# A depthwise convolution over two streams: the taps of both in one instruction, and eight of 31 on the tensor engine

## The chip, the cores and the metric

The kernel runs on one NeuronCore of a Trainium2 chip. Its engines work side by side from their own instruction queues: TensorE (matrix products; PE in the profile, PEld for its weight loads), VectorE (DVE), ScalarE (ACT), GpSimd (POOL) and SyncE (SP, which here issues the DMAs). The metric is the device time of one execution in microseconds, taken as the median of several runs.

## The reference, cut to what matters

The program is a whole model in float32: a block with two layers (a latent stream of 512 tokens and a context stream of 256 tokens, width 1024) and behind it a second block with two layers. The change lies in the first mixer of the first block. It projects both streams, and a quarter of the projection goes through a depthwise convolution of width 31 over time, each stream by itself with zeros at its ends:

```python
def conformer_conv(p_glu, conv_w, conv_b, ln_g, ln_b):
    a, gate = jnp.split(p_glu, 2, axis=-1)
    u = depthwise_conv(a * jax.nn.sigmoid(gate), conv_w, conv_b)   # 31 taps, 512 channels
    return jax.nn.silu(layer_norm(u, ln_g, ln_b))
```

Its result and that of a differential attention are put side by side and projected back to width 1024. The convolution is thus 31 multiplications and additions for each of 512 channels and 768 tokens; its result is first needed by the output projection, which comes after the attention has begun.

## The kernel before

**Layout.** Channels lie on the 128 partitions, tokens along the free axis. The 512 convolution channels are four blocks (`i` = 0 to 3), the two streams are `regs` (`r` = 0: 512 columns, `r` = 1: 256 columns). The convolution's input `us` holds, for each block, both streams in one row of 828 columns, each with 15 zeros on either side, so that stream 1 begins 30 columns later than in an array without zeros. Large products are made in three passes (lines 90 to 92): weights and activations are split into a high half and a low remainder (`whi`, `wlo`), the high half cast by ScalarE (line 73), the low one subtracted by VectorE or GpSimd (line 74).

**The stages around the change.** First come the gate gemms (lines 412 to 424): for each block, two gemms per stream give gate and value, and VectorE writes `us` (line 420) and starts the result `conv` with the first tap and the bias (line 421). The filters of a later Hyena layer (`hyena_filters`) are made in the same stage. Then the loop of line 488 makes eight query/key gemms, each followed on VectorE by three instructions of a rotation (lines 493 to 495); the loop of line 500 makes the value gemms. Between these, one step at a time by `next(tg)`, runs the generator `taps` (line 436), and after its eight steps the four of `conv_norm` (line 456, layer norm and activation). Attention follows (from line 539), with the first half of the output projection as filler (`out_gemm(0, ...)`), which reads the convolution's result.

**The taps.** For each block and stream: ScalarE multiplies taps 30 and 29 into two buffers, GpSimd adds these, VectorE does taps 1 to 28 one after the other in place, and GpSimd adds its part:

```python
for j in range(1, 29):
    nc.vector.scalar_tensor_tensor(out=o, in0=u[:, j:j + n], scalar=cw[:, i, j:j + 1], in1=o,
                                   op0=ALU.mult, op1=ALU.add)                    # lines 448 to 450
nc.gpsimd.tensor_tensor(out=o, in0=o, in1=o2, op=ALU.add)                        # line 451
```

**The modulation.** While the query/key and value weights are loaded, `wsplit` (line 60) also advances a generator (`k.mods`, line 141): eight weights of 512 KB per kind, each with two products into 32 of the 128 rows of one accumulator (line 153), a copy by ScalarE (line 157), a second accumulator (line 160) and an addition by VectorE (line 161). Its weights and those of the gemms share three raw buffers (`wraw`, lines 66 and 149).

**Order.** Each engine works through its queue in a fixed order. The framework writes that order when the program is built: it goes through the instructions by their order in the program as priority, with a time model of its own, and lets a later instruction go first where an earlier one cannot start yet in that model. So taps are mixed into the gate stage too. On the chip the order stays as written, even where the times come out otherwise.

**Accumulators.** PSUM has eight banks. Lines 370, 371, 374 and 485 deal them out: four for the gemms (`evps`), two for the modulation (`evmps`), two for the Hyena filters and, after these, for the norm of the convolution (`evcps`). The pool `evp` (line 435) opens when the Hyena filters' pools are closed and reuses their memory, a tile at a time.

Of the kernel before, what the change touches and what calls it, by code (L numbers as in the profile page):

```python
# [10 lines left out]
F32 = mybir.dt.float32  # L11
# [15 lines left out]
def f32(ap):  # L27
    return ap.bitcast(F32)

# [325 lines left out]
def even_mixer(k, xc):  # L355
# [10 lines left out]
    with ExitStack() as es:  # L366
# [3 lines left out]
        ps = hp.enter_context(k.pool("evps", 4, space=PSUM))  # L370
        mps = hp.enter_context(k.pool("evmps", 2, space=PSUM))
        lam = cp.tile([128, 1], F32, name="lam")
        conv = [k.tmp([128, TC], "conv", F32, 4, cp) for i in range(4)]
        with k.pool("hyf") as hy, k.pool("evf", 2, space=PSUM) as fps:
# [5 lines left out]
            with k.pool("evn") as np_:  # L380
                rbs = [k.norm_stats([t], [rg], ps, np_)[0] for t, rg in zip((xl, xc), regs)]
                with k.pool("ada", side="right") as mp:
                    for i, _ in enumerate(chain(k.mods(0, 1, mps, mp, 12), k.mods(0, 0, mps, mp, 12))):
                        if i == 3:
                            next(fg)
                h1 = hp.enter_context(k.pool("evh", side="right"))
                hh = h1.tile([128, 8, TC], F32R, name="hh")
                hl = h1.tile([128, 8, TC], F32R, name="hl")
                h = (hh, hl)
                k.norm([xl, xc], regs, [k.mgain(0, 1, G_N1, r) for r in range(2)], [k.mcol(0, 0, r) for r in range(2)], hh, hl, ps, np_, rbs)  # L390
# [14 lines left out]
            with k.pool("evu") as pp:  # L405
# [6 lines left out]
                for i in range(4):  # L412
                    ws = [k.wsplit(a["ev_w_fm"][i * 2 + j]) for j in range(2)]
                    for r, (c0, n) in enumerate(regs):
# [6 lines left out]
                        nc.vector.tensor_scalar(out=conv[i][:, c0:c0 + n], in0=us[:, i, u0 - 15:u0 - 15 + n], scalar1=cw[:, i, 0:1],  # L421
                                                scalar2=cb[:, i:i + 1], op0=ALU.mult, op1=ALU.add)
                        next(fg, None)
                    next(fg, None)
# [9 lines left out]
        qk = [b3() for i in range(8)]  # L434
        with k.pool("evp") as pp, k.behind([k.mods(0, kind, mps) for kind in (2, 3, 4)], 2):
            def taps():

                for i in range(4):
                    for r, (c0, n) in enumerate(regs):
                        u = us[:, i, c0 + 30 * r:c0 + 30 * r + 30 + n]  # L440
                        o = conv[i][:, c0:c0 + n]
                        o2 = k.tmp([128, T], "cv2", bufs=2, pool=tp_)[:, :n]
                        nc.scalar.mul(o2, u[:, 30:30 + n], cw[:, i, 30:31])
                        for j in (29,):
                            o3 = k.tmp([128, T], "cv3", bufs=2, pool=tp_)[:, :n]
                            nc.scalar.mul(o3, u[:, j:j + n], cw[:, i, j:j + 1])
                            nc.gpsimd.tensor_tensor(out=o2, in0=o2, in1=o3, op=ALU.add)
                        for j in range(1, 29):
                            nc.vector.scalar_tensor_tensor(out=o, in0=u[:, j:j + n], scalar=cw[:, i, j:j + 1], in1=o,
                                                           op0=ALU.mult, op1=ALU.add)  # L450
                        nc.gpsimd.tensor_tensor(out=o, in0=o, in1=o2, op=ALU.add)
                        yield
                for r in range(2):
                    yield from conv_norm(r)

            def conv_norm(r):
                c0, n = regs[r]
                cs = [conv[i][:, c0:c0 + n] for i in range(4)]
# [26 lines left out]
            cps = hp.enter_context(k.pool("evcps", 2, space=PSUM))  # L485
# [53 lines left out]
        with k.pool("eva") as pp, k.pool("evaps", 2, space=PSUM) as ps, k.pool("evop", 1, space=PSUM) as op_, k.pool("evgp", 1, space=PSUM) as gp, \  # L539
# [88 lines left out]
            for i in range(4):  # L628
                k.split(conv[i], mix[2 * i], mix[2 * i + 1])
# [3 lines left out]
            for u, (hd, c0, k0) in enumerate(units):  # L633
# [4 lines left out]
                if u % 3 == 0:  # L638
                    os_ = k.tmp([128, TC], "conv", F32, 4, cp)
# [1609 lines left out]
```

## Time and profile before

| | |
|---|---|
| median of 3 runs | 3670.63 us (3670.61 to 3671.2) |
| the profiled execution | 3667.19 us |
| its span, first to last instruction | 3665.4 us |
| mean granted clock of TensorE | 0.970 |
| TensorE busy | 3410.3 us |
| VectorE busy | 2439.1 us |
| ScalarE busy | 1464.3 us |
| GpSimd busy | 680.0 us |

The span is what the profile shows; the time of the execution has 1.8 us more around it. The profile names an instruction by its line, engine, operation and tiles (output <- inputs), with partitions x elements. Times of a timeline are from the span's start. A granted clock of 1.0 is 2.4 GHz, 0.5 is 1.2 GHz. A product of float32 operands shows as two records of TensorE. The convolution's stage lies between 75 and 370 us of the span; everything behind it is as long as ten such stages.

### The profile page before, as it was taken

How to read it: one execution, taken by the hardware profiler on the slowest of the kernel's cores; microseconds unless marked ns; L12 is line 12 of the kernel's file. 1: busy time of each engine (PE TensorE's matmuls, PEld its weight loads, DVE VectorE, ACT ScalarE, POOL GpSimd, SP SyncE). 2: the span in 40 equal slices, each digit the busy share in tenths (PEclk: the TensorE clock that was granted, in tenths of full speed). 3: DMA queues.
4: the chain of work that ended last, by engine and by line, in shares of the span. 5: the costliest groups of instructions: out<-in, count | busy, mean ns of one | idle time of the engine just before them, and what ended most of it. 6: DMA issues, size and time to landing. Idle time of an engine off the chain costs nothing.

```text
span 3665.4 us, 55031 instructions
## 1 busy us (share of the span) xinstructions
PE 3410.3 (93%) x21924; PEld 2813.6 (77%) x21924; DVE 2439.1 (67%) x4107; ACT 1464.3 (40%) x2529; POOL 680.0 (19%) x595
## 2 busy tenths in 40 slices
PE   6985989999998899889999999999999989999999
PEld 3764878888887666567888887767998777777998
DVE  7998877554448855654333676667877676758886
ACT  4212643213226434323223444544444554644443
POOL 0034201002102432311111032022111032012110
PEclk9997999999999999989999999999999999999999
DMA  6333113333333222422222313332333313242333
GB/s 212 109 127 93 48 50 117 119 125 118 120 111 110 89 71 78 125 97 81 92 93 97 107 59 101 97 121 83 103 106 97 116 50 115 77 132 83 102 98 98
DMA packets 156843, 369.32 MB, mean 101 GB/s; under 512 B 19207, under 2 KB 44167, under 8 KB 156200
## 3 DMA queue, kind: packets, MB, share of 16 engines
q1 hardware_dynamic: 156584, 365.79, 31.3%
q8 instruction: 172, 2.82, 0.3%
q14 instruction: 87, 0.71, 0.1%
HBM read 334.27 MB, written 28.31 MB: 99 GB/s over the span
## 4 chain that ended last, share of the span: by engine, by line
PE 39%; DVE 14%; issue 7%; ACT 4%; POOL 2%; DMA 2%; SPq 0%; DVEq 0%; POOLq 0%; ACTq 0%
PE acc L90 11%; PE acc L92 11%; PE acc L91 10%; DVE wlo L74 2%; DMA wraw<-in_w_up_dram 2%; DVE wslo L85 1%; DVE hb L1612 1%; ACT whi L73 1%; PE rec L1337 1%; PE rec L1338 1%; DVE ws L1920 1%; PE rec L1322 1%; DVE oz L828 1%; ACT mp L1847 0%; DVE xl L2023 0%
## 5 line engine op out<-in xcount | busy, mean ns | idle before, releaser
L73 ACT CAST whi<-wraw 128x1024 fp32r<-128x1024 f32 (+2 forms) x442 | 408.0, 924 | 843.3 <-PE acc L91 652.9
L74 DVE TENSOR_TENSOR wlo<-wraw,whi 128x1024 fp32r<-128x1024 f32 (+2 forms) x438 | 490.5, 1120 | 184.7 <-ACT whi L73 180.5
L90 PE MATMUL acc<-hh,whi 128*128 128x512 f32 (+1 forms) x1024 | 367.2, 359 | 10.8 <-ACT whi L73 7.6
L92 PE MATMUL acc<-hh,wlo 128*128 128x512 f32 (+1 forms) x1024 | 364.4, 357 | 6.9 <-DVE wlo L74 4.0
L91 PE MATMUL acc<-hl,whi 128*128 128x512 f32 (+1 forms) x1024 | 365.6, 357 | 2.5 <-DVE hl L256 2.1
L91 PE MATMUL acc<-hidl,whi 128*128 128x512 f32 (+1 forms) x768 | 274.3, 357 | 2.9 <-DVE hidl L85 2.9
L90 PE MATMUL acc<-hidh,whi 128*128 128x512 f32 (+1 forms) x768 | 274.6, 358 | 0.0
L92 PE MATMUL acc<-hidh,wlo 128*128 128x512 f32 (+1 forms) x768 | 274.2, 357 | 0.0
L341 POOL TENSOR_TENSOR sqr<-relu 128x512 f32<-128x512 f32 (+1 forms) x96 | 126.6, 1319 | 688.9 <-ACT relu L339 675.6
L90 PEld LDWEIGHTS acc<-hh,whi 128*128 128x128 f32 x1024 | 195.9, 191 | 49.9 <-ACT whi L73 11.5
L92 PEld LDWEIGHTS acc<-hh,wlo 128*128 128x128 f32 x1024 | 195.4, 191 | 39.9 <-DVE wlo L74 6.1
L91 PEld LDWEIGHTS acc<-hl,whi 128*128 128x128 f32 x1024 | 196.5, 192 | 35.8 <-DVE hl L256 5.6
L92 PE MATMUL acc<-shh,wlo 128*128 128x512 f32 (+1 forms) x480 | 193.6, 404 | 7.6 <-DVE wlo L74 7.6
L90 PE MATMUL acc<-shh,whi 128*128 128x512 f32 (+1 forms) x480 | 195.6, 407 | 3.5 <-ACT whi L73 3.5
L91 PE MATMUL acc<-shl,whi 128*128 128x512 f32 (+1 forms) x480 | 194.1, 404 | 0.2 <-issue 0.2
L85 POOL TENSOR_TENSOR flo<-fth,fhi 128x512 fp32r<-128x512 f32 x44 | 84.9, 1931 | 530.1 <-ACT fhi L84 473.6
L90 PE MATMUL acc<-fsh,wshi 128*128 128x256 f32 x576 | 163.5, 284 | 4.5 <-ACT wshi L84 4.5
L91 PEld LDWEIGHTS acc<-hidl,whi 128*128 128x128 f32 x768 | 145.5, 189 | 26.9 <-DVE hidl L85 3.4
L191 DVE SCALAR_TENSOR_TENSOR mdacc<-wraw,cs,mdacc 128x1024 f32<-128x1024 f32 x70 | 94.4, 1372 | 103.7 <-DMA wraw<-in_ada_w_dram 103.6
L91 PE MATMUL acc<-fsl,wshi 128*128 128x256 f32 x576 | 163.2, 283 | 0.0
L90 PEld LDWEIGHTS acc<-hidh,whi 128*128 128x128 f32 x768 | 144.8, 188 | 23.5
L92 PEld LDWEIGHTS acc<-hidh,wlo 128*128 128x128 f32 x768 | 144.8, 189 | 23.2
(684 smaller groups left out, 9167.8 us busy)
## 6 DMA issues: line engine op xcount, KB each, us to landing
wraw<-in_mlp_w_dram SPq DMA_DIRECT2D x128, 512.0 KB, 3.5
wraw<-in_ada_w_dram SPq DMA_DIRECT2D x96, 512.0 KB, 4.0
wraw<-in_w_in_dram SPq DMA_DIRECT2D x58, 512.0 KB, 3.5
wraw<-in_od_w_fm_dram SPq DMA_DIRECT2D x36, 512.0 KB, 3.5
wraw<-in_w_gate_dram SPq DMA_DIRECT2D x72, 256.0 KB, 2.9
wraw<-in_w_up_dram SPq DMA_DIRECT2D x72, 256.0 KB, 3.1
wraw<-in_w_down_dram SPq DMA_DIRECT2D x48, 256.0 KB, 2.7
wraw<-in_w_down_dram SPq DMA_DIRECT2D x32, 320.0 KB, 3.0
```

What stands on the lines that cost most here:

```text
L73: nc.scalar.copy(hi, raw)
L74: (eng or nc.vector).tensor_tensor(out=lo, in0=raw, in1=f32(hi), op=ALU.subtract)
L85: (eng or nc.vector).tensor_tensor(out=lo, in0=src, in1=f32(hi), op=ALU.subtract)
L90: nc.tensor.matmul(out, s[0], m[0], start=first, stop=False)
L91: nc.tensor.matmul(out, s[0], m[1], start=False, stop=False)
L92: nc.tensor.matmul(out, s[1], m[0], start=False, stop=last)
L191: nc.vector.scalar_tensor_tensor(out=acc, in0=w, scalar=c, in1=acc, op0=ALU.mult, op1=ALU.add)
L341: nc.gpsimd.tensor_tensor(out=s, in0=r, in1=r, op=ALU.mult)
L828: nc.vector.scalar_tensor_tensor(out=o, in0=p[:, j:j + n], scalar=w[:, j:j + 1], in1=o, op0=ALU.mult, op1=ALU.add)
L1322: nc.tensor.matmul(vn_ps[pf[d], hd], wT[:, c, pf[d]], S[:, c], start=True, stop=True)
L1337: nc.tensor.matmul(op_[pf[d], hd], qd[:, c, pf[d]], S[:, c], start=True, stop=False)
L1338: nc.tensor.matmul(op_[pf[d], hd], at[pf[d], c], vn[pf[d], hd], start=False, stop=True)
```

## The change

The result `conv` gets 798 columns instead of 768, so that it lies like the input: both streams with 30 columns between them, which are computed and never read. One tap is then one instruction over both streams. Taps 1 to 20 stay with VectorE, 29 and 30 with ScalarE and GpSimd, and taps 21 to 28 (`P0, PT = 21, 8`) go to TensorE. For these GpSimd makes, per block and tap, a matrix of 128 x 32 (`dia`) that holds a 32x32 diagonal for each quarter of the channels. `strips` multiplies each quarter `q` of the channels by its diagonals into its own bank; four taps `s` go to the four quarters of the bank's rows, and two rounds of 16 products accumulate. ScalarE copies the four banks out, and `joined` sums the four taps of each bank by four products with a 128x32 matrix of ones on the diagonals (`k.sum4`); VectorE adds that to `conv`.

The banks are dealt anew: three for the gemms, two for the modulation at first and one afterwards (`evmps1`), four for the strips and the norm. The buffers of the ScalarE taps move to the pool `evp`, and the first tap with the bias is done once per block over both streams. Readers of `conv` take its columns per stream.

```diff
-        ps = hp.enter_context(k.pool("evps", 4, space=PSUM))
-        mps = hp.enter_context(k.pool("evmps", 2, space=PSUM))
+        ps = hp.enter_context(k.pool("evps", 3, space=PSUM))
+        W = TC + 30
+        conv = [k.tmp([128, W], "conv", F32, 4, cp) for i in range(4)]
...
-                with k.pool("ada", side="right") as mp:
+                with k.pool("ada", side="right") as mp, k.pool("evmps", 2, space=PSUM) as mps:
...
-                        nc.vector.tensor_scalar(out=conv[i][:, c0:c0 + n], in0=us[:, i, u0 - 15:u0 - 15 + n], scalar1=cw[:, i, 0:1],
-                                                scalar2=cb[:, i:i + 1], op0=ALU.mult, op1=ALU.add)
                         next(fg, None)
+                    nc.vector.tensor_scalar(out=conv[i], in0=us[:, i, 0:W], scalar1=cw[:, i, 0:1], scalar2=cb[:, i:i + 1], op0=ALU.mult, op1=ALU.add)
...
+        mps = hp.enter_context(k.pool("evmps1", 1, space=PSUM))
+        cps = hp.enter_context(k.pool("evcps", 4, space=PSUM))
...
+            dia = pp.tile([128, 4, PT, 32], F32, name="cdia")
+            for i in range(4):
+                nc.gpsimd.tensor_tensor(out=dia[:, i], in0=k.sum4.unsqueeze(1).to_broadcast([128, PT, 32]),
+                                        in1=cw[:, i, P0:P0 + PT].unsqueeze(2).to_broadcast([128, PT, 32]), op=ALU.mult)
+            def strips(i, r):
+                c0, n = regs[r]
+                bank = [k.tmp([128, 512], "acc", pool=cps, bufs=None) for _ in range(4)]
+                for t in range(0, PT, 4):
+                    for s in range(4):
+                        for q in range(4):
+                            p = slice(32 * q, 32 * q + 32)
+                            u0 = c0 + 30 * r + P0 + t + s
+                            nc.tensor.matmul(bank[q][32 * s:32 * s + 32, :n], dia[p, i, t + s], us[p, i, u0:u0 + n], start=t == 0, stop=t + 4 >= PT)
+                e = k.tmp([128, 4, T], "cve", bufs=1, pool=pp)
+                for q in range(4):
+                    nc.scalar.copy(e[:, q, :n], bank[q][:, :n])
+                return i, r, e
+            def joined(i, r, e):
+                c0, n = regs[r]
+                acc = k.tmp([128, 512], "acc", pool=ps, bufs=None)[:, :n]
+                for q in range(4):
+                    nc.tensor.matmul(acc[32 * q:32 * q + 32], k.sum4, e[:, q, :n], start=True, stop=True)
+                o = conv[i][:, c0 + 30 * r:c0 + 30 * r + n]
+                nc.vector.tensor_tensor(out=o, in0=acc, in1=o, op=ALU.add)
             def taps():
                 for i in range(4):
...
+                    u = us[:, i]
+                    o = conv[i]
+                    o2 = k.tmp([128, W], "cw2", bufs=2, pool=pp)
+                    nc.scalar.mul(o2, u[:, 30:30 + W], cw[:, i, 30:31])
+                    for j in (29,):
+                        o3 = k.tmp([128, W], "cw3", bufs=1, pool=pp)
+                        nc.scalar.mul(o3, u[:, j:j + W], cw[:, i, j:j + 1])
+                        nc.gpsimd.tensor_tensor(out=o2, in0=o2, in1=o3, op=ALU.add)
+                    last = None
+                    for j in range(1, P0):
+                        nc.vector.scalar_tensor_tensor(out=o, in0=u[:, j:j + W], scalar=cw[:, i, j:j + 1], in1=o, op0=ALU.mult, op1=ALU.add)
+                        if j == 10:
+                            last = strips(i, 0)
+                            yield
+                    nc.gpsimd.tensor_tensor(out=o, in0=o, in1=o2, op=ALU.add)
+                    joined(*last)
+                    last = strips(i, 1)
+                    yield
+                    joined(*last)
                 for r in range(2):
                     yield from conv_norm(r)
...
             for i in range(4):
-                k.split(conv[i], mix[2 * i], mix[2 * i + 1])
+                for r, (c0, n) in enumerate(regs):
+                    k.split(conv[i][:, c0 + 30 * r:c0 + 30 * r + n], mix[2 * i][:, c0:c0 + n], mix[2 * i + 1][:, c0:c0 + n])
```

## Rows read from the trace of the kernel before

**Rows 1.** The page's first part: busy us (share of the span) and instructions by engine.
```profile
PE 3410.3 (93%) x21924; PEld 2813.6 (77%) x21924; DVE 2439.1 (67%) x4107; ACT 1464.3 (40%) x2529; POOL 680.0 (19%) x595
```
**Rows 2.** Windows: length, then busy us of PE, PEld, DVE, ACT, POOL; clock, DMA share, GB/s.
```profile
75.00:170.00 95.00, 85.78 (x430) 67.54 (x429) 88.00 (x136) 32.13 (x50) 11.07 (x7) 0.95 0.28 92
170.00:187.00 17.00, 17.00 (x81) 12.41 (x80) 16.84 (x29) 4.57 (x6) 1.29 (x1) 1.00 0.59 201
187.00:270.00 83.00, 74.90 (x410) 57.91 (x409) 81.21 (x126) 14.10 (x22) 30.03 (x16) 0.94 0.38 125
270.00:320.00 50.00, 11.26 (x31) 3.98 (x31) 50.00 (x77) 8.77 (x12) 30.61 (x11) 0.55 0.26 70
320.00:367.00 47.00, 45.29 (x345) 42.05 (x346) 31.69 (x60) 17.70 (x35) 9.92 (x10) 0.93 0.39 125
```
**Rows 3.** The same windows for the tap line L449 alone: VectorE's busy time.
```profile
75.00:170.00 95.00, 30.87 (x47) 0.95 0.28 92
170.00:187.00 17.00, 3.32 (x7) 1.00 0.59 201
...
sum 292.00, DVE 145.62; mean DVE 29.12
```
**Rows 4.** Waits of TensorE, 187 to 367 us: for whom, us, times, the longest.
```profile
PE acc L91 <- DVE wlo L74: 26.2, 2, 24.4
PE acc L153 <- DMA wraw<-in_ada_w_dram: 9.4, 4, 3.7
PE acc L90 <- DVE rt L494: 3.9, 2, 3.5
PE acc L92 <- POOL wlo L74: 3.0, 3, 1.9
```
**Rows 5.** VectorE in order of time, 291 to 316 us: start, us, what, how many.
```profile
291.60 19.07 DVE L449 SCALAR_TENSOR_TENSOR conv<-xl,c_ev_conv_w,conv 128x512 f32<-128x512 f32 x34
...
312.54 2.82 DVE L74 TENSOR_TENSOR wlo<-wraw,whi 128x1024 fp32r<-128x1024 f32 x1
```
**Rows 6.** Groups by line and shape, 75 to 367 us: busy us, mean ns of one.
```profile
L449 DVE SCALAR_TENSOR_TENSOR conv<-xl,c_ev_conv_w,conv 128x512 f32<-128x512 f32 x112 | 91.1, 813 | 0.0
L449 DVE SCALAR_TENSOR_TENSOR conv<-xl,c_ev_conv_w,conv 128x256 f32<-128x256 f32 x112 | 67.2, 600 | 0.1
```
**Rows 7.** The line L449 by itself: ns shortest/median/longest, first and last start.
```profile
L449 DVE SCALAR_TENSOR_TENSOR conv<-xl,c_ev_conv_w,conv x224: 468/736/2867, 85.9 to 330.3; 128x256 f32<-128x256 f32 x60, 128x512 f32<-128x512 f32 x52
```
**Rows 8.** VectorE in order of time: a tap and the start of its neighbour.
```profile
175.57 0.47 DVE L449 SCALAR_TENSOR_TENSOR conv<-xl,c_ev_conv_w,conv 128x256 f32<-128x256 f32 x1
175.97 0.68 DVE L703 TENSOR_TENSOR hys<-hyf,hyf 128x512 f32<-128x512 f32 x1
```
**Rows 9.** Groups by line and shape, 187 to 367 us: reads of PSUM by VectorE, ScalarE.
```profile
L498 ACT COPY b<-acc 128x256 f32<-128x256 f32 x8 | 2.9, 368 | 11.3 <-PE acc L92 11.3
L470 DVE TENSOR_TENSOR conv<-conv,acc 128x512 f32<-128x512 f32 x4 | 2.5, 682 | 0.7 <-PE acc L121 0.7
L157 ACT COPY wraw<-acc 128x512 f32<-128x512 f32 x3 | 1.8, 586 | 17.9 <-issue 14.1 <-PE acc L153 3.8
L470 DVE TENSOR_TENSOR conv<-conv,acc 128x256 f32<-128x256 f32 x4 | 1.4, 417 | 1.8 <-PE acc L121 1.8
```
**Rows 10.** TensorE in order of time: products that use a part of the array.
```profile
161.45 1.05 PE L153 MATMUL acc<-wraw,cs 128*32 128x512 f32 x4
...
196.25 1.06 PE L153 MATMUL acc<-wraw,cs 128*32 128x512 f32 x8
...
1225.53 0.75 PE L1237 MATMUL prep<-R,LM 32*32 32x32 f32 x64
```
**Rows 11.** SyncE's queue, 172 to 178 us; DMA issues 120 to 375 us (us to landing).
```profile
172.74 0.33 SPq L70 DMA_DIRECT2D wraw<-in_ev_w_fm_dram  x1
...
wraw<-in_ev_w_fm_dram SPq DMA_DIRECT2D x8, 512.0 KB, 4.9
```
**Rows 12.** VectorE in order of time: the norm's last products.
```profile
369.14 0.75 DVE L482 SCALAR_TENSOR_TENSOR conv<-cv,conv 128x256 f32<-128x256 f32 x2
```

More of the change, by code (lines that the diff above doesn't have):

```diff
@@ L28, in f32 @@
     return ap.bitcast(F32)
+P0, PT = 21, 8
 class K:
@@ L369, in even_mixer @@
         tp_ = hp.enter_context(k.pool("evt", side="right"))
-        ps = hp.enter_context(k.pool("evps", 4, space=PSUM))
-        mps = hp.enter_context(k.pool("evmps", 2, space=PSUM))
+        ps = hp.enter_context(k.pool("evps", 3, space=PSUM))
         lam = cp.tile([128, 1], F32, name="lam")
-        conv = [k.tmp([128, TC], "conv", F32, 4, cp) for i in range(4)]
+        W = TC + 30
+        conv = [k.tmp([128, W], "conv", F32, 4, cp) for i in range(4)]
         with k.pool("hyf") as hy, k.pool("evf", 2, space=PSUM) as fps:
@@ L436, in taps @@
             def taps():
                 for i in range(4):
[L439 to L452, printed above, removed]
+                    u = us[:, i]
@@ L457, in conv_norm @@
                 c0, n = regs[r]
-                cs = [conv[i][:, c0:c0 + n] for i in range(4)]
+                cs = [conv[i][:, c0 + 30 * r:c0 + 30 * r + n] for i in range(4)]
                 sm = k.tmp([128, T], "cv2", bufs=2, pool=tp_)[:, :n]
@@ L483, in conv_norm @@
                 yield
-            cps = hp.enter_context(k.pool("evcps", 2, space=PSUM))
             tg = taps()
@@ L638, in even_mixer @@
                 if u % 3 == 0:
-                    os_ = k.tmp([128, TC], "conv", F32, 4, cp)
+                    os_ = k.tmp([128, W], "conv", F32, 4, cp)
                 values(hd, now, os_, c0, k0)
```

## The prediction

> **What bounds the kernel now.** First view: busy time by engine [rows 1]. TensorE is busy 93% of the 3665.4 us, VectorE 67%; as an average it names no limit for the convolution. The chain of waits does not reach back to it either (its shares add up to some 70% of the span, and its pieces lie later), so I go by stretches [rows 2]. The reader is to see that the order turns round: from 187 to 320 us VectorE is busy 131.2 of 133 us, and from 270 to 320 TensorE works 11.3 of 50 us, at a granted clock of 0.55, that is mostly on the lower level (1.2 GHz). Next, what VectorE does there: the tap line takes 145.6 us between 75 and 367 us, of which 34.2 us lie before 187 [rows 3], as filler beside the gate gemms and the Hyena filters. Last, the waits of TensorE from 187 to 367 us [rows 4]: 26.2 us for the low half of a weight that VectorE computes. Why that half is late stands in VectorE's order [rows 5]: 34 taps, 19 us long, run ahead of it, and the subtraction comes only at 312.5 us. So the stretch from 187 to 367 us, 180 us long, is set by VectorE's taps first and by TensorE's gemms at its ends.
>
> **VectorE.** Removed are 224 taps, 112 over 512 and 112 over 256 columns. Their means are 813 and 600 ns [rows 6], the shortest 468 ns and the median 736 ns [rows 7]; I read 468 as an undisturbed tap of 256 and 736 as one of 512. That is 268 ns for 256 columns, so one tap over 798 columns takes 736 + 286 x 268/256 = 1035 ns. Neighbours overlap by 70 ns: after a tap of 470 ns the next instruction starts 400 ns later [rows 8]. Undisturbed, the taps of now would take 112 x (0.736 + 0.468) - 224 x 0.07 = 119 us; 145.6 us are measured, so 26 us are disturbance, which I put down to GpSimd's work beside them. Added are 80 taps: 80 x (1.035 - 0.07) = 77 us undisturbed. GpSimd keeps a similar load: it loses eight adds at 512 and eight at 256 and gets eight at 798 and four small products for the diagonals. So the disturbance lies between 0 and 26 us; I take 20, near the present. Added too are eight additions of the tensor engine's part, 4 x 0.68 + 4 x 0.42 = 4.4 us [rows 9]. The first tap (four calls for eight) is even. Sum: 145.6 - 77 - 20 - 4.4 = 44 us less (bounds 38 and 64).
>
> If the lead before 187 us stays, VectorE's 162.9 us from 187 to 367 [rows 2] become 119 us.
>
> **TensorE.** Added, per channel block and stream: 32 products of 32x32 in two rounds of 16, then four of 128x32. The trace has the latter shape: two products over 512 columns (two records each, two column groups) are done in 1.05 us, and four of them, in all four column groups, in 1.06 [rows 10], so the column groups run beside one another. That prices the joining at 1.06 us for 512 and about 0.55 us for 256 columns: 4 x 1.6 = 6.4 us. A round of 16 tiles over 512 columns is not in the trace. Lower bound: all 16 run together like those, two rounds 2.0 us, and 1.0 us for 256 columns: 4 x 3.0 = 12 us. Upper bound: only the column groups overlap and the four row groups follow one another: 7.3 and 3.7 us, 44 us in all. The nearest row is a run of 32 products of 32x32 over 32 columns on four tiles that differ in row and column, done in 0.75 us (64 records) [rows 10]: tiles in different row groups do overlap. I take 12 us. With the joining 18.4 us; the upper end is 50 us.
>
> The Trainium skill ("TensorE: Matmul & The Clock Gate", Part 3: Packing small matmuls) gives 10.6 times, not 16, for 16 tiles of 32x32. No row here has 16 tiles; by that figure an estimate of the rounds would be 12 x 16/10.6 = 18 us, and the saving 6 us smaller than the sum below.
>
> TensorE's present work from 187 to 367 us is 131.5 us busy [rows 2]. Part of it ran on the low clock: nearly all of the 11.3 us between 270 and 320, and about an eighth of the time before and after (0.94 and 0.93). At the high level it would be some 9 us shorter (bounds 0 and 14). So 122 + 18 = 140 us.
>
> What of its 48.5 us of idle time stays? The 26.2 us for the late half go, for VectorE, with 119 us of work, is no longer behind; so do the 3.9 us for a bank that VectorE had not emptied, and part of the 9.4 us for weights of the modulation [rows 4], whose buffers waited for the same subtractions. The 3.0 us for GpSimd's halves and the rest stay: I take 12 us (bounds 8 and 20).
>
> **Banks and buffers.** The gemms' accumulators go from four to three banks, the modulation's from two to one, and the strips get four. Between 75 and 187 us the gate gemms lose a bank; TensorE idles 9.2 us there now [rows 2], and with three a bank has the two 256-column gemms to be emptied in. Taken at nothing, bounds -2 and +5. The modulation's one bank opens after the Hyena filters' banks are free, at about 187 us; now its first product runs at 161.5 us [rows 10]. Its two weights then hold two of the three raw buffers until 187, and the weights of the second query/key gemm, now requested at 172.7 us, follow after that: with 4.9 us to land [rows 11] and some 2.3 us to be split they come at about 194 us, where the gemm started at 188. The first strips can fill part of the gap: 3 us taken, 0 to 8 as bounds.
>
> **Beside other work.** ScalarE gets 32 copies out of the strips' banks, 16 x 0.586 + 16 x 0.368 = 15.3 us [rows 9], and loses about 2 us of multiplications. It is busy 40.6 of 180 us [rows 2], so its capacity hides them; their order is a risk, for the cast of the next weight can stand behind a copy that waits for the strips. GpSimd's four diagonal products are under 1 us each and done before the first strip; they cost what the strips then start later, while the query/key gemms run. SyncE's queue: the reload of x still waits for the last reader of the convolution's input, now also the last strips; it is needed only by the first output gemm, after 367 us. The splits of the convolution's result become eight for four, about 1 us more beside TensorE's attention. The split after the norm hangs on the norms of the convolution: last tap at 330.3 us [rows 7], the norm's last product at 369.9 [rows 12], a tail of 39 us. With VectorE through at 187 + 119 = 306 us, the norm's own work included, the tail ends before TensorE does.
>
> **Sum.** 140 + 12 + 3 = 155 us for 180: 25 us less, rounded down to 24 for what the strips' changes of shape cost. The profiled execution took 3667.2 us; it becomes 3643. The median of the runs is 3.4 us above it, so the forecast is 3647 us. Its own range, by the bounds above, is 3634 to 3661.
>
> **Rivals.**
> 1. TensorE without gaps: VectorE's end of the backlog also takes the waits for weights, 187 + 140 and little more: 40 us less, 3630. For it: nearly all waits in [rows 4] name VectorE or a buffer it held. Against: GpSimd's halves and the weights' landing remain. 0.15.
> 2. The tail of the convolution sets the end. A wide tap needs both streams of its block, and if the lead before 187 us is lost by that, all 97 us of taps and the 4 us of additions lie behind it, where 111 us of taps lie now: the last tap 10 us earlier than now, and the norms 39 us behind it. Then the stage ends 10 us earlier: 3661. For it: the last block's input comes late, and 187 us is near. Against: now 54 of 224 taps find room before it. 0.13.
> 3. Banks (the other side): the joined product takes one of only three gemm banks and keeps it until taps, GpSimd's addition and VectorE's addition are through. Then each query/key step works with two, and its next gemm waits until VectorE has turned the last one out. Such a wait is 3.5 us at its longest now, of 3.9 us in two [rows 4]; one in each of eight steps is 28 us, more than the 24 gained: +4 us, 3675. It decides once the plan puts the joined product ahead of the taps that it waits for. For it: VectorE's order is fixed ahead and runs late by long runs of taps. Against: 54 taps are done before 187 us. 0.10.
> 4. It doesn't pack: the 16 tiles run four at a time. The rounds cost 44 us, 32 more than taken: +8 us, 3679. 0.07. Against it stands the 32x32 run [rows 10].
>
> The forecast itself: 0.55. The range reaches from 3619 (rival 1 with its spread) to 3673 and leaves out most of rival 4, half of rival 3 and the far end of rival 1. A difference under 0.2%, 7 us, cannot be told from none. Faster takes the forecast and rivals 1 and 2 except for their last few hundredths: 0.79. Within 0.2% lie half of rival 3, some of rival 4 and what misses: 0.10. Slower: 0.11.
>
> **What would show it.** Right: no run of TensorE idle for over 10 us between 187 and the start of attention, the granted clock above 0.9 throughout, taps near 1.0 us each, 95 to 105 us of taps in all, a round of 16 tiles in about 1 us, attention's first scores at about 343 us. Wrong: strips of over 5 us each; waits of the gemms for the rotation's reads or for the joined additions adding up to over 10 us; VectorE still at 10 of 10 when TensorE has stopped; or a later stage that takes the time back.

## The result, and the profile after: 33 us slower

| | before | after |
|---|---|---|
| median | 3670.62 us (4 runs, 3669.0 to 3671.2) | 3703.84 us (4 runs, 3698.56 to 3706.59) |
| ratio | | 1.0088, 95% interval 1.0076 to 1.0100 |
| the profiled execution, its span | 3667.2, 3665.4 us | 3706.6, 3704.8 us |
| attention's first scores (end of the stage) | 366.8 us | 381.8 us |
| from there to the end of the span | 3298.6 us | 3323.0 us |

The forecast was 3647 us. Profile against profile 39.4 us are lost: 15.0 up to attention's first scores, where 24 were to be gained, and 24.4 behind them, where nothing was expected. In medians it is 33.2 us: the profiled execution of before lies 3.4 us under its median and that of the change 2.8 us above its own, so some 6 us of the 39.4 are scatter. The ratios in this text leave out two slow runs, one of the kernel before (3840.22 us) and one of wide20 (4322.93 us), at granted clocks of 0.83 and 0.71. In the changed kernel's line numbers the taps are L487, the strips L458, ScalarE's copies L461, the joining L469, VectorE's addition of it L471, the rotation L535 to L537, the gemms L94 to L96, the weights' halves L77 and L78, the first scores L612.

The page's first part, answering [rows 1]; TensorE has 576 records more:
```profile
PE 3442.8 (93%) x22500; PEld 2830.0 (76%) x22500; DVE 2403.3 (65%) x3971; ACT 1474.6 (40%) x2557; POOL 669.5 (18%) x591
```
The windows of the stage after the change, columns as in [rows 2]:
```profile
75.00:170.00 95.00, 85.00 (x431) 68.29 (x431) 86.90 (x115) 28.31 (x42) 2.93 (x3) 0.96 0.24 78
170.00:187.00 17.00, 13.05 (x53) 9.89 (x52) 16.52 (x20) 3.43 (x5) 7.88 (x6) 0.94 0.37 124
187.00:270.00 83.00, 58.91 (x512) 38.19 (x511) 78.38 (x79) 19.79 (x34) 31.54 (x13) 0.84 0.30 99
270.00:320.00 50.00, 49.33 (x519) 34.75 (x517) 15.91 (x27) 11.65 (x24) 12.29 (x7) 0.99 0.29 93
320.00:382.00 62.00, 51.55 (x378) 43.02 (x378) 25.49 (x43) 24.73 (x42) 18.11 (x12) 0.89 0.51 156
```
The reader is to see two halves. Up to 270 us VectorE is busy 78.4 of 83 us and TensorE idles 24; from 270 to 320 us TensorE works 49.3 of 50 us and VectorE 15.9. In [rows 2] it was the other way round: TensorE was busy first and starved between 270 and 320. The strips and their joining lie in both halves, 11.1 us of them before 270 us, 11.1 up to 320 and 0.6 behind.

What TensorE waited for from 187 to 382 us, answering [rows 4]:
```profile
PE acc L94 <- DVE rt L536: 8.5, 3, 5.0
PE acc L96 <- DVE wlo L78: 7.9, 2, 6.9
PE acc L157 <- DMA wraw<-in_ada_w_dram: 6.3, 2, 3.4
PE acc L107 <- POOL cv L517: 6.2, 1, 6.2
PE acc L157 <- DVE mods L165: 2.9, 1, 2.9
```
Of the 24.1 us up to 270 us, 20.7 are waits for VectorE. VectorE in order of time shows why the first two wait: runs of taps stand ahead of the rotation and of a low half, as in [rows 5], only earlier. Five taps take 8.1 us (five undisturbed ones are 4.8), and fourteen stand before the rotation at 260 us:
```profile
197.10 8.11 DVE L487 SCALAR_TENSOR_TENSOR conv<-xl,c_ev_conv_w,conv 128x798 f32<-128x798 f32 x5
205.14 0.73 DVE L535 STREAM_SHUFFLE rt<-acc 128x512 f32<-128x512 f32 x1
...
209.28 2.88 DVE L78 TENSOR_TENSOR wlo<-wraw,whi 128x1024 fp32r<-128x1024 f32 x1
...
243.75 16.47 DVE L487 SCALAR_TENSOR_TENSOR conv<-xl,c_ev_conv_w,conv 128x798 f32<-128x798 f32 x14
...
260.15 0.73 DVE L535 STREAM_SHUFFLE rt<-acc 128x512 f32<-128x512 f32 x1
```
The tap line by itself, answering [rows 7] (ns shortest/median/longest, first and last start):
```profile
L487 DVE SCALAR_TENSOR_TENSOR conv<-xl,c_ev_conv_w,conv x80: 1029/1044/2693, 90.6 to 259.2; 128x798 f32<-128x798 f32 x80
```
TensorE's new work by line and shape from 75 to 390 us (busy us, mean ns), and three pieces of it in order of time, answering [rows 10]:
```profile
L458 PE MATMUL acc<-xl,cdia 32*32 32x512 f32 x256 | 10.0, 638 | 0.0
L458 PE MATMUL acc<-xl,cdia 32*32 32x256 f32 x256 | 6.0, 385 | 0.0
...
L469 PE MATMUL acc<-cve,sum 128*32 128x512 f32 x32 | 4.3, 604 | 0.0
```
```profile
201.67 2.96 PE L458 MATMUL acc<-xl,cdia 32*32 32x512 f32 x64
...
222.34 1.07 PE L469 MATMUL acc<-cve,sum 128*32 128x512 f32 x8
223.34 1.50 PE L458 MATMUL acc<-xl,cdia 32*32 32x256 f32 x64
```
SyncE's queue, answering [rows 11]: the weights of the second query/key gemm are asked for at 197.6 us instead of 172.7.
```profile
170.64 0.33 SPq L74 DMA_DIRECT2D wraw<-in_ev_w_fm_dram  x1
...
197.62 0.42 SPq L74 DMA_DIRECT2D wraw<-in_ev_w_fm_dram  x1
```

### The profile page after: what moved, and what is told of

Read it like the earlier page. It is cut to its first block, busy times and chain, and to the rows that moved or that the text cites. A ratio compares the mean times of both kernels' runs of the same rounds, so it can differ in the third digit from the quotient of the medians.

```text
span 3704.8 us, 56098 instructions
## 1 busy us (share of the span) xinstructions
PE 3442.8 (93%) x22500; PEld 2830.0 (76%) x22500; DVE 2403.3 (65%) x3971; ACT 1474.6 (40%) x2557; POOL 669.5 (18%) x591
## 4 chain that ended last, share of the span: by engine, by line
PE 38%; DVE 14%; issue 7%; ACT 4%; DMA 2%; POOL 2%; SPq 0%; DVEq 0%; POOLq 0%; ACTq 0%
PE acc L94 11%; PE acc L96 11%; PE acc L95 10%; DVE wlo L78 2%; DMA wraw<-in_w_up_dram 2%; DVE wslo L89 1%; ACT whi L77 1%; DVE hb L1655 1%; PE rec L1380 1%; PE rec L1381 1%; DVE ws L1963 1%; DVE wlo L89 1%; PE rec L1365 1%; DVE oz L871 1%; ACT mp L1890 0%
## 5 line engine op out<-in xcount | busy, mean ns | idle before, releaser
L77 ACT CAST whi<-wraw 128x1024 fp32r<-128x1024 f32 (+2 forms) x442 | 408.1, 924 | 857.9 <-PE acc L95 647.6
L78 DVE TENSOR_TENSOR wlo<-wraw,whi 128x1024 fp32r<-128x1024 f32 (+2 forms) x438 | 489.3, 1118 | 191.3 <-ACT whi L77 187.0
L94 PE MATMUL acc<-hh,whi 128*128 128x512 f32 (+1 forms) x1024 | 369.4, 361 | 19.1 <-DVE rt L536 8.5
L96 PE MATMUL acc<-hh,wlo 128*128 128x512 f32 (+1 forms) x1024 | 366.4, 359 | 18.0 <-DVE wlo L78 18.0
L96 PE MATMUL acc<-hidh,wlo 128*128 128x512 f32 (+1 forms) x768 | 274.2, 357 | 0.3 <-DVE wlo L78 0.3
L94 PE MATMUL acc<-hidh,whi 128*128 128x512 f32 (+1 forms) x768 | 274.4, 357 | 0.0
L94 PEld LDWEIGHTS acc<-hh,whi 128*128 128x128 f32 x1024 | 197.0, 192 | 58.0 <-ACT whi L77 10.8
L96 PEld LDWEIGHTS acc<-hh,wlo 128*128 128x128 f32 x1024 | 196.6, 192 | 52.7 <-DVE wlo L78 21.5
L96 PE MATMUL acc<-shh,wlo 128*128 128x512 f32 (+1 forms) x480 | 194.7, 406 | 8.5 <-DVE wlo L78 8.5
L94 PE MATMUL acc<-shh,whi 128*128 128x512 f32 (+1 forms) x480 | 196.0, 408 | 3.5 <-ACT whi L77 3.5
L94 PE MATMUL acc<-fsh,wshi 128*128 128x256 f32 x576 | 164.0, 285 | 4.3 <-ACT wshi L88 4.3
L96 PE MATMUL acc<-fsh,wslo 128*128 128x256 f32 x576 | 162.6, 285 | 1.4 <-DVE wslo L89 1.4
L96 PEld LDWEIGHTS acc<-hidh,wlo 128*128 128x128 f32 x768 | 144.3, 188 | 23.6 <-DVE wlo L78 0.7
L94 PEld LDWEIGHTS acc<-hidh,whi 128*128 128x128 f32 x768 | 144.3, 188 | 23.2
```

What stands on the lines that cost most here:

```text
L77: nc.scalar.copy(hi, raw)
L78: (eng or nc.vector).tensor_tensor(out=lo, in0=raw, in1=f32(hi), op=ALU.subtract)
L94: nc.tensor.matmul(out, s[0], m[0], start=first, stop=False)
L96: nc.tensor.matmul(out, s[1], m[0], start=False, stop=last)
```

## The experiments

Two numbers are read from each profile: the start of attention's first scores, which closes the stage, and the time from there to the end of the span. Single runs of one kernel scatter by up to 12 us about their median, so the ratio to the kernel before on the same chip stands beside it. The two numbers come from one execution each. The framework can write another order for each kernel, so a difference between two of them is the edit with the order that came with it.

| kernel | median us | ratio (95%) | first scores | rest of span |
|---|---|---|---|---|
| before | 3670.62 | | 366.8 | 3298.6 |
| the change | 3703.84 | 1.0088 (1.0076-1.0100) | 381.8 | 3323.0 |
| early_bank | 3699.31 | 1.0081 (1.0064-1.0098) | 380.6 | 3317.2 |
| banks_only | 3678.11 | 1.0021 (1.0011-1.0031) | 371.5 | 3299.5 |
| wide_only | 3662.13 | 0.9975 (0.9962-0.9988) | 352.4 | 3303.7 |
| no_strips | 3664.13 | 0.9983 (0.9973-0.9994) | 355.4 | 3303.4 |
| strips_twice | 3711.92 | 1.0121 (1.0107-1.0136) | 392.3 | 3325.1 |
| wide20 | 3653.16 | 0.9955 (0.9942-0.9967) | 343.3 | 3301.4 |
| wide30 | 3658.69 | 0.9971 (0.9961-0.9982) | 356.4 | 3300.5 |
| no_join | 3693.44 | 1.0060 (1.0048-1.0072) | 384.8 | 3308.2 |
| no_strips_early | 3662.42 | 0.9970 (0.9960-0.9979) | 353.4 | 3307.2 |
| before_pad | 3690.98 | 1.0058 (1.0044-1.0072) | 370.9 | 3319.1 |
| pad_end | 3682.03 | 1.0026 (1.0015-1.0038) | 366.9 | 3315.8 |
| pad_72 | 3673.70 | 1.0006 (0.9997-1.0015) | 368.7 | 3305.4 |
| pad_32 | 3686.44 | 1.0033 (1.0021-1.0045) | 366.7 | 3316.2 |
| pad_64 | 3669.28 | 0.9994 (0.9986-1.0003) | 366.7 | 3300.8 |
| after_pad_32 | 3693.38 | 1.0056 (1.0043-1.0069) | 382.3 | 3308.0 |
| after_pad_224 | 3699.93 | 1.0074 (1.0061-1.0088) | 387.5 | 3308.4 |

### The stage: bank, taps, strips

**early_bank.**
```diff
         ps = hp.enter_context(k.pool("evps", 3, space=PSUM))
+        mps1 = hp.enter_context(k.pool("evmps1", 1, space=PSUM))
...
-        mps = hp.enter_context(k.pool("evmps1", 1, space=PSUM))
```


> The changed kernel (3704 us, 33 us slower than before), with the modulation's one bank opened at the start of the mixer instead of after the Hyena filters. Theory Ring (my favourite): the modulation's first product waits for that bank (194 us instead of 161 us), its weights hold two of three raw buffers meanwhile, and the weights of the second query/key gemm are asked for 25 us late; with the bank open early they are asked for at about 173 us again, and some 20 of the 25 us come back: 3684 us, 3678 to 3690. Theory Taps: VectorE's wide taps set the stage whenever the weights come: 3700 to 3706. Theory Strips: the strips and their joining on TensorE (25 us) are what is added: 3700 to 3706. Of the 20 us that are lost behind the stage, where every engine has the same instructions in the same order: if they belong to the program (its 576 more records of TensorE, its place in memory), the time from attention's first scores to the end stays at 3323 us; if they follow from when the stage ends, it falls towards the 3298.6 us of before.

The weights are asked for at 176.7 us, 21 us earlier, and the first scores come only 1.2 us earlier. VectorE reaches the first rotation at 205.0 us as it did (205.1): the late weights were hidden behind VectorE. My favourite, Ring, falls; the median is 0.7 us under what Taps and Strips expect. The rest of the span stays long (3317.2 us).

**banks_only.**
```diff
-        ps = hp.enter_context(k.pool("evps", 4, space=PSUM))
-        mps = hp.enter_context(k.pool("evmps", 2, space=PSUM))
+        ps = hp.enter_context(k.pool("evps", 3, space=PSUM))
...
+        mps = hp.enter_context(k.pool("evmps1", 1, space=PSUM))
+        cps = hp.enter_context(k.pool("evcps", 4, space=PSUM))
```


> The kernel before with only the accumulators dealt as in the changed one (three for the gemms, two then one for the modulation, four for the norm's pool); taps as before. Ring: the second query/key gemm comes some 25 us late, but VectorE, which sets this stage there, works on its taps meanwhile, so the stage ends only 3 to 12 us later: 3674 to 3683. Taps and Strips: nothing that costs is in it, 3669 to 3672. From attention's first scores to the end: 3298 to 3300 us if the loss behind the stage belongs to the larger program, up to 3323 if it goes with the banks.

The stage ends 4.7 us later, the median is 0.21% up: inside Ring's range, but for another reason, as early_bank says. TensorE idles 13.2 us from 75 to 187 us, for 9.2 in [rows 2].

**wide_only.**
```diff
-                        for j in range(1, 29):
-                            nc.vector.scalar_tensor_tensor(out=o, in0=u[:, j:j + n], ...
+                    for j in range(1, 29):
+                        nc.vector.scalar_tensor_tensor(out=o, in0=u[:, j:j + W], ...
+                        if j == 14:
+                            yield
```


> The kernel before with only the wide taps (28 per block over 798 columns on VectorE, no strips), banks as before. Ring: 112 taps at 0.965 us and 20 us of disturbance are 128 us for 146, VectorE sets the stage, so it ends some 15 us earlier: 3650 to 3660. Taps: a wide tap needs both streams of its block, the lead before 187 us is lost, and GpSimd's longer additions disturb more: 3668 to 3690. Strips: as Ring. From attention's first scores to the end: as before, 3298 to 3300 us.

The first scores come 14.4 us earlier, as Ring expected; the median falls by 0.25%, to 2 us above its range. The half of the change that widens the taps gains by itself and beats both kernels. Theory Taps falls.

**no_strips and wide20.** Both leave taps 21 to 28 out; they differ only in the banks.
```diff
-                    for j in range(1, 29):
+                    for j in range(1, P0):
```


> The changed kernel with TensorE's eight taps left out (no diagonals, no strips, no copies, no joining, so taps 21 to 28 are missing from the result). Strips: their 18 + 7 us on TensorE go, 3676 to 3682. Ring: the late weights stay; the strips that lie in TensorE's waits cost nothing there, so 12 to 18 us go: 3686 to 3692. Taps: nothing goes, 3700 to 3706. From attention's first scores to the end: 3298 to 3300 us if the loss behind the stage belongs to the 576 more records of TensorE, 3323 if to the banks or the wide result.

> The wide taps alone with the banks of before, and taps 21 to 28 left out altogether (their part is missing from the result): VectorE loses 32 x 0.965 = 31 us against the wide taps alone (3662 us), TensorE gets nothing. If VectorE still sets the end of the stage once the taps are wide, 15 to 30 us go: 3632 to 3647. If it does not (TensorE's own work and the weights do), almost nothing goes: 3655 to 3664. Against the kernel without the strips but with the new banks (3664 us) it gives the price of the banks: 0 to 5 us.

Each kernel's window from 187 us to its first scores, columns as in [rows 2], no_strips first:
```profile
187.00:355.40 168.40, 139.63 (x818) 106.83 (x817) 120.05 (x138) 43.00 (x66) 64.66 (x32) 0.91 0.41 133
```
```profile
187.00:343.30 156.30, 129.56 (x775) 104.18 (x774) 118.93 (x135) 42.86 (x68) 62.26 (x32) 0.89 0.41 133
```
The same VectorE work (120 and 119 us), yet the new banks have 10 us more of TensorE's work behind 187 us and end 12.1 us later, where wide20's expectation had 0 to 5. From wide_only to wide20, 31 us of VectorE's taps are worth 9.1 us at the first scores: VectorE is still a limit, with less than a third of its time, and wide20's median lies between its two ranges. And the strips, with their joining, cost 26.4 us (355.4 to 381.8), for 22.8 us that they keep TensorE busy; all three theories on no_strips expected less of it (3676 us at the least, 3664.1 measured). TensorE is busy 20.0 us longer with them and idle 6.4 us longer. The first half of no_strips, to be held against the same window above, has less idle time than with the strips:
```profile
187.00:270.00 83.00, 66.49 (x338) 47.83 (x337) 82.82 (x82) 16.41 (x21) 38.58 (x15) 0.92 0.38 124
```

**no_strips_early.** no_strips with the bank opened early (the edit of early_bank).

> The changed kernel without its strips (first scores at 355.4 us) and with the modulation's one bank opened at the start of the mixer. The same taps with the banks of before have their first scores at 343.3 us, so the dealing of the banks costs 12 us there. Theory Late (the bank that opens only behind the Hyena filters holds back the weights of the second query/key gemm): the 12 us come back, first scores at 343 to 347 us, 3651 to 3656 us in median. Theory Few (it is one bank less for the gemms and one for the modulation): nothing comes back, 352 to 357 us, 3660 to 3666.

2.0 of the 12.1 us come back, so Few holds: it is one bank less for the gemms and for the modulation, or the order that the framework writes for it.

**strips_twice.**
```diff
-                for t in range(0, PT, 4):
+                for t in (0, 4, 0, 4):
```


> The changed kernel with the strips' 32 products done twice over (the second time starting each bank anew, so the result is the same): 17.8 us more of TensorE (8 times 2.96 or 1.50 us). Theory Path (TensorE's added work lands on the path whole, for VectorE no longer sets the end of the stage): 3704 + 18 = 3722 us, 3716 to 3727. Theory Gaps (the strips fill TensorE's waits, and the loss comes from the waits themselves): 3704 to 3711. Behind the stage the changed kernel loses another 10 to 16 us against the kernel before, from 2350 us on, with the same order of instructions: if that goes with the number of TensorE's instructions, another 10 or so come on top; if not, nothing.

The first scores come 10.5 us later. The strips are busy 30.0 us for 16.0, so 14.0 us are added (the 17.8 of the expectation took the 2.96 us of the first one for all). Three quarters of the added work land on the path; the median lies between the ranges of Path and Gaps, at the edge of Gaps. The rest of the span does not grow a second time (3325.1 for 3323.0).

**no_join.** `joined` and its calls are left out, `strips` stays.

> The changed kernel with the strips and ScalarE's copies kept, but without the joining (32 products and VectorE's 8 additions left out, so taps 21 to 28 are missing from the result). Theory Work: only the 6.9 us of TensorE's joining go, and attention's first scores come 4 to 7 us earlier, at 375 to 378 us (381.8 in the changed kernel). Theory Bank (a rival of the prediction): the joined product holds one of only three gemm banks until VectorE adds it, and the gemms wait for the others; without it the waits of the gemms for the rotation's reads (8.5 us) go too and the first scores come 12 to 16 us earlier, at 366 to 370 us. In median: 3697 to 3700 or 3688 to 3692 us.

The first scores come 3.0 us later instead of earlier, and the median, 3693.4 us, lies between the two ranges. TensorE no longer waits for the rotation, but 12.3 us for low halves and 12.1 us for the modulation's addition: the framework wrote another order. On Work against Bank this decides nothing. It decided something else, below.

**wide30.** wide_only, and VectorE does taps 29 and 30 too; the lines with `cw2` and `cw3` are gone.

> The wide taps alone with the banks of before, and VectorE does all of taps 1 to 30: ScalarE's two multiplications and GpSimd's two additions per block are gone. 8 more taps are 7.7 us of VectorE; the 116 taps of the kernel with the wide taps alone took 143 us for 119.5 undisturbed (1.03 us each), so 23 us are disturbance. Theory Contention (GpSimd's additions cause most of that): VectorE's taps take 124 to 132 us, the rotations and low halves come earlier, 3648 to 3659 us. Theory Work (the disturbance comes from elsewhere): 7.7 us more on VectorE, 3662 to 3670.

VectorE's 120 taps take 137.7 us, the 112 of wide_only 136.0: at 1.03 us undisturbed that leaves 14 and 21 us of disturbance, so GpSimd's additions, with ScalarE's multiplications that go with them, made some 6 us of it. Contention expected taps of 124 to 132 us. The stage ends 4.0 us later than in wide_only, as Work says. The median lies in Contention's range, but the ratios of the two kernels overlap: neither theory holds as it stands.

### Behind the stage: the same order, 24 us longer

The change brings no new instruction there; from the end of the first mixer on all five queues hold the same instructions in the same order. Of the 24.4 us, 5.3 fall between the first and the last scores (120.0 and 125.3 us), 19.1 behind these.

**before_pad**, and with other numbers or places **pad_72**, **pad_end**, **pad_32**, **pad_64**:
```diff
+        pad = [k.tmp([128, 512], "acc", pool=ps, bufs=None) for _ in range(4)]
+        for n in range(288):
+            p, m = slice(32 * (n % 4), 32 * (n % 4) + 32), slice(32 * (n // 4 % 4), 32 * (n // 4 % 4) + 32)
+            nc.tensor.matmul(pad[n % 4][m, :16], k.ones[p, :32], k.ones[p, :16], start=True, stop=True)
         conv = [k.tmp([128, TC], "conv", F32, 4, cp) for i in range(4)]
```


> The kernel before with 288 idle products of 32x32 over 16 columns (576 records of TensorE, as many as the strips and their joining have) put at the very start, where TensorE waits for its first weights; nothing else is changed, and all engines keep their order. It may cost 0 to 8 us at the start. Theory Program (the 10 to 16 us that the changed kernel loses from 2350 us on go with the greater number of TensorE's instructions or their place in memory): 8 to 16 us more from 520 us to the end, 3680 to 3692. Theory Other (they come from what the strips leave behind, or from elsewhere): none there, 3669 to 3679.

The old kernel with 576 idle records at its start loses 4.1 us up to the first scores and 20.5 behind them. So a loss of this size, greater than theory Program expected (8 to 16), comes without anything that the strips compute.

> The kernel before with the 288 idle products put at the very end, behind the last gemm, instead of at the start; they may cost 0 to 15 us there. With them at the start, the time from 520 us to the end was 20.9 us longer. Theory Size (a larger program is placed otherwise in memory, and all transfers of weights are slower): the same 15 to 21 us between 520 us and the last gemm. Theory Position (the instructions behind the added ones come to lie elsewhere in TensorE's instruction stream): nothing there, up to 3 us.

The added products stand between the old last gemm and the end, 14.5 us before the end of the span where that gemm had ended 4.2 before it. That is 10.3 us, and the median is up by 8.7 (3673.33 for before on that chip): nothing is left over, so it is not size. (The profiled execution by itself is 7 us longer up to the last gemm; it is 2.5 us above its median, the one of before 3.4 below its own.)

> The kernel before with 72 idle products (144 records) at the start instead of 288. If the loss behind goes with the number, a quarter of the 20.9 us: 4 to 6 us from 520 us to the end. If it hangs on where the later instructions come to lie, or on a threshold of size, any value from 0 to 21 us, not a quarter. If it is chance, 0.

1.9 us at the start; the rest is 6.8 us longer in the profile, the median only 0.06% up. Not told apart from the scatter, and no quarter could be. But no_join had 512 records more, nearly as many as the change, and a rest of 3308.2 us. The runs with the loss had 576, 576, 576 and 1088 more: each 64 beyond a multiple of 128. That made a guess that could be put to the test.

> The kernel before with 32 idle products (64 records of TensorE) at the start. Theory Place (the loss behind the stage comes whenever the number of added records is 64 beyond a multiple of 128): the whole loss for next to no work, 14 to 20 us, 3684 to 3691 us. Theory Number (it comes from some 550 records on): 0 to 3 us, 3669 to 3674.

> The kernel before with 64 idle products (128 records) at the start. Place: nothing is lost, 3669 to 3675 us. Number: the same, 3669 to 3675; if this one loses and the 64 records do not, neither holds.

The page of each (its first and third lines), and the row of the first scores, pad_32 first:
```profile
span 3682.9 us, 55163 instructions
...
PE 3422.1 (93%) x21988; PEld 2823.0 (77%) x21988; DVE 2440.5 (66%) x4107; ACT 1464.3 (40%) x2529; POOL 678.9 (18%) x595
```
```profile
L574 PE MATMUL S<-KS,QS x80: 277/393/792, 366.7 to 489.2; 128*128 128x256 f32 x48, 128*128 128x512 f32 x32
```
```profile
span 3667.5 us, 55293 instructions
...
PE 3412.3 (93%) x22052; PEld 2816.0 (77%) x22052; DVE 2441.7 (67%) x4107; ACT 1464.7 (40%) x2529; POOL 681.4 (19%) x595
```
```profile
L574 PE MATMUL S<-KS,QS x80: 274/386/776, 366.7 to 486.6; 128*128 128x256 f32 x48, 128*128 128x512 f32 x32
```
Both start attention at 366.7 us, as the kernel before does. The one with 64 idle records then takes 15.4 us longer than the one with 128; in medians 17.2. Place holds, Number falls.

**after_pad_32, after_pad_224.** The same loop in the changed kernel, in a pool of four banks of its own.

> The changed kernel with 32 idle products (64 records) more at its start, 640 in all, a multiple of 128 and not of 512. Place, if 128 is the step: the loss behind the stage goes, 14 to 18 us, 3685 to 3691 us. Place, if 512 is the step: it may stay. Number: 3703 to 3707.

> The changed kernel with 224 idle products (448 records) more at its start, 1024 in all, a multiple of 128 and of 512. They may cost 0 to 4 us at the start, as the 288 did in the kernel before (4 us). Place: the loss behind the stage goes, 3687 to 3694 us. Number: it stays or grows, 3704 to 3712.

With 32 products that compute nothing of use the changed kernel becomes 10 us faster by its median (3693.4; by the ratios 0.32%, some 12 us), all of it behind the stage: 3308.0 for 3323.0. Its median is 2 us above Place's range and 10 below Number's. With 224 the rest is 3308.4 us, but the products cost 5.7 us ahead of the first scores; the median, 3699.9 us, lies between the two ranges, and by its ratio alone this kernel is not told apart from the changed one.

## Why the prediction was wrong, point by point

**VectorE's work: right.** Taps of 1044 ns in the median for 1035; 92.9 us of them in all for 97. From 187 us to the first scores VectorE is busy 119.6 us, for 119 foreseen.

**The step that failed:** "The 26.2 us for the late half go, for VectorE, with 119 us of work, is no longer behind". With 119 us of work VectorE is behind all the same, because the work lies in front: it is busy for 94% of the time up to 270 us, the taps run ahead of rotations and low halves, and TensorE idles 24 us there, 20.7 of them for VectorE. Idle from 187 us to the first scores are 35.2 us (194.8 less 159.6 busy), not 12. A sum over the stage cannot see that. In the first half VectorE sets the time, in the second TensorE. wide20 against wide_only and no_strips against the change measure both sides of the exchange: 31 us less for VectorE bring 9.1 us, 22.8 us more for TensorE cost 26.4. Half of that work (11.1 us) stands in the first half, and it does not fill the gaps there: without it TensorE idles 16.5 us up to 270 us and does 66.5 us of other work, with it 24.1 and 47.8. What is not done there comes behind 270 us, where TensorE has no slack. Why the gaps stay open beside the strips, by their place in the order or by the bank of the joined product, no run separates.

**The sum.** The 155 us became 194.8: 23.2 more idle and 19.6 more busy, without the 3 for the late weights. Of the 19.6, 9.3 are the clock's gain that did not come, 5.5 grown work, 4.8 the strips and their joining. The stated range was narrower than its own bounds: the upper ones for the clock (9), the idle time (8), the late weights (5) and the banks (5) add up to 27 us, 3674, and the measured time lies beyond that too.

**The strips: mis-sized.** 2.35 us (the first 2.96) and 1.50 us for a block and stream, where 2.0 and 1.0 were taken; 16.0 us in all for 12. The joining is 6.8 us for 6.4. The Trainium skill ("TensorE: Matmul & The Clock Gate", Part 3: Packing small matmuls) gives 10.6 times for 16 tiles. The prediction's estimate of 18 us by it was nearer to the 16.0 measured than the 12 taken.

**The clock: no gain in busy time.** The granted clock, a mix of its two levels (1.0 is 2.4 GHz, 0.5 is 1.2), fell to 0.84 between 187 and 270 us (0.94 before) and rose to 0.99 from 270 to 320 (0.55): the low stretches moved with TensorE's idle time. Without strips and joining TensorE is busy 136.8 us, for 131.3 before and 122 foreseen.

**Three gemm banks: at the upper bound.** TensorE idles 13.9 us from 75 to 187 us instead of 9.2: 4.7 us, taken at nothing with 5 as bound. That work comes behind 187 us instead and is most of the 5.5 us that TensorE's own work has grown by there.

**The late weights (3 us): the mechanism came, the cost did not.** They are asked for 25 us later, but early_bank shows that VectorE covers it.

**The stage in runs, step by step** (first scores): wide taps with 28 on VectorE, 366.8 to 352.4; taps 21 to 28 out of VectorE, to 343.3; the banks dealt anew, to 355.4; the strips that replace these taps, to 381.8. The first two gain 23.5 us, nearly the 24 of the forecast; the last two take 38.5.

**The rivals.** No gaps (1): TensorE idled 35.2 us. Tail (2): the norm's products end 4.6 us behind the first scores, before 3.1 us behind; not the bound. Banks (3) named the price of the joined product; waits for the rotation's reads are 8.5 us, not 28, and no_join could not tell whose they are. That the banks cost 12 us in their dealing itself, it did not see. Packing (4): the tiles do pack.

**Behind the stage.** No step and no rival had it: 10 to 15 us of the 33 come with the number of TensorE's records ahead of the later layers, by what it leaves over a multiple of 128 (pad_32, after_pad_32). The 5.3 us between first and last scores stay open; wide_only (127.0 us there for 120.0) has them, wide30 (120.2), with the same wide result, has not.

## What to carry to other kernels

Where two engines set a stage in turns, sum each half for itself and ask in which half the moved work lands and whether it fills gaps there, not whether the totals fit. Price the parts of a change one by one: here the first alone (wider taps, 0.25 to 0.29% faster) beats the whole. And before a small loss is put down to a mechanism far from the edit, put idle instructions into the old kernel: what they alone do to the time belongs to no idea in the change.

## What the runs showed of the hardware that was not expected

64 records of TensorE that compute nothing, at the start of an otherwise unchanged program with the same order on all five queues, made it 15 us longer from 367 us to the end (ratio 1.0033, 1.0021 to 1.0045); 128 made no difference (0.9994, 0.9986 to 1.0003). In five kernels with 64 beyond a multiple of 128 the rest of the span is 3316.2 to 3325.1 us; in those with a multiple of 128 (0, 128, 512, 640, 1024) it is 3298.6 to 3308.4. Each of these is one execution; corrected by how far that execution lies from its kernel's median, the two groups stay apart, at 3317 to 3320 and 3300 to 3311 us. The kernel with 144 records (16 beyond) has 3305.4 us; the one with the records at the end, behind all else, is left out of this.

The step of 128 has a counterpart in the traces. The page's third part lists a queue for instructions, q8, with 172 packets of 16 KB (2.82 MB) before. Its packets are 172 with 64 records more, 173 with 128, 176 with 512 and 576, 177 with 640, 180 with 1024 and 1088: one for 128 records with their weight loads. And in each of the five kernels TensorE stops for 2.0 or 2.1 us within the same run of small products, for nothing that the profile shows ("issue"). The other kernels have no pause in it. pad_32, then pad_64:
```profile
2123.18 1.16 PE L1649 MATMUL acc<-hP 128*32 128x32 f32 x113
2126.34 0.32 PE L1649 MATMUL acc<-hP 128*32 128x32 f32 x13 [2.01 <-issue]
```
```profile
2114.63 1.27 PE L1649 MATMUL acc<-hP 128*32 128x32 f32 x126
```
In pad_32 a packet of q8 is under way from 2124.0 to 2124.9 us, as the pause begins. That TensorE waits there for instructions is likely, but no run shows it. Such pauses are a part of the loss only: behind the first scores they add up to 9.9 us in pad_32 and 5.3 in pad_64. For the same 20460 records there TensorE is busy 9.7 us longer (3140.7 for 3131.1) and idle the other 5.7, at a granted clock of 0.966 for 0.970 in the mean of the execution. The second block's gate weights land later too, in the median after 3.1 to 3.3 us in the five kernels and 2.9 to 3.0 in the others; what that costs is not shown. Nor does a run here show whether the step is 128 in other programs.
